# Starting the rotary tables earlier and pacing them by the attention that runs beside them

## The chip, the cores and the metric

The kernel runs on one core of one Trainium2 chip. The metric is device time in microseconds (us), the median of several runs. TensorE (PE in the profile) does the matrix products, VectorE (DVE) and ScalarE (ACT) the element-wise work, GpSimd (POOL) a share of it, and every transfer is issued from SyncE's queue (SP).

## What is computed

Two layers of a decoder trunk over 1024 positions of width 1024. Each layer normalises x, projects it to the inputs of eight heads of 256 (four mLSTM heads, four retention heads), runs them chunk by chunk, and projects back. Only the retention heads need the rotary tables, which depend on nothing but the positions:

```python
def rotary(t, positions):
    inv_freq = 1.0 / (ROPE_BASE ** jnp.linspace(0.0, 1.0, d // 2))
    ang = positions.astype(jnp.float32)[..., None] * inv_freq
    cos, sin = jnp.cos(ang), jnp.sin(ang)
    t1, t2 = jnp.split(t, 2, axis=-1)
    return jnp.concatenate([t1 * cos - t2 * sin, t2 * cos + t1 * sin], axis=-1)

def reference(...):
    for l in range(DEPTH):
        h = rmsnorm(x, norm_g[l]) * (1.0 + scale) + shift
        mq, mk, mv, mo, mz, mi, mf, rq, rk, rv, rz = split_cols(h @ w_in[l])
        ...   # y_m: four mLSTM heads from mq, mk, mv, mi, mf, gated by mo and mz
        ret = retention_chunkwise(rotary(rq, positions), rotary(rk, positions), rv)
        y_r = head_layernorm(ret) * silu(rz)
        x = x + gate * (concat(y_m, y_r) @ w_out[l])
    return rmsnorm(x, final_g)
```

## The kernel before

Float32 products are made of three products of split halves (`mm3`, lines 145 to 147): each operand is rounded to a high part by ScalarE (`split_to`, L621) and the rest is taken by GpSimd or VectorE (L622).

The program is written as generators. `run_units` runs the projections in the foreground; one step of it (a unit, some 12 to 24 matmuls) ends with `tick()`. `launch(gen, delay)` puts a background generator on a list, and each `tick` lets those that are due run to their next `yield n`, which asks for n ticks of rest. In this way an attention's products are dealt out among the next head's projections. TensorE's instructions stand in the order in which the program issues them (`manual_schedule` for PE). The order of the other engines' instructions is chosen by the build's scheduler, which may move an instruction ahead of its place in the program once its inputs are there; on the chip each engine then works its queue strictly in that order.

A head passes through `gate_path` (its z and o projections, evacuated by L550 and L560), `qk_ml` (q and k with a short convolution on VectorE, L636 to L644, and k's copies through memory, L663 to L673), `v_path` (values, split at L607 and L608) and `attention`. One round of an attention makes scores (matmuls L772; VectorE multiplies them by the decay matrix at L786, L787, L789 or L796, L797), values (L845, L855, then L859, L871 and `normalise`), and the update of the state: products into PSUM, added by VectorE into `cf` (L825), rounded by ScalarE to `cH` (L621), the rest by VectorE to `cL` (L622). The next round's values (L855) on TensorE wait for both.

PSUM banks of the pools `pp` (projections) and `pa` (attention), four each, are handed on in turn, so a matmul into a bank also waits for whoever read it last.

`rotary_tables` works in four rounds of 256 positions. A round loads the positions to all partitions (L381), makes the angle and its fraction of a turn in 26 instructions of VectorE on tiles of 128 x 256 (L383 to L407), and stores two results to memory (L410, `rdr`). It holds three of the six buffers named `g`. Its results are read back by `load_rotary` (L735) at the end of head 3's attention. It is launched once, in layer 0, behind head 1's values; head 1's attention is launched ahead of those values with a delay of 7 ticks.

Of the kernel before, what the change touches and what calls it, by code (L numbers as in the profile page):

```python
# [13 lines left out]
I32 = mybir.dt.int32  # L14
# [5 lines left out]
P = 128  # L20
# [8 lines left out]
CH = 256  # L29
# [38 lines left out]
def two_pi_split():  # L68
    c = 1.0 / (2.0 * math.pi)

    def top(v):
        m, e = math.frexp(v)
        return math.ldexp(round(m * 4096.0) / 4096.0, e)

    c1 = top(c)
    c2 = top(c - c1)
    return c1, c2, float(np.float32(c - c1 - c2))
# [3 lines left out]
def tile_hybrid_trunk(ctx, tc, x, xt, c, positions, w_ada, b_ada, norm_g, w_in, conv_w, conv_b,  # L81
                      b_igate, b_fgate, gn_m, gn_r, w_out, final_g, consts, out):
    nc = tc.nc
    V, A, G, PE, Q = nc.vector, nc.scalar, nc.gpsimd, nc.tensor, nc.sync
# [20 lines left out]
    def wt(tag, n, bufs, dt=F32):  # L105
        return wrk.tile([P, n], dt, tag=tag, bufs=bufs, name=nm(tag))
# [13 lines left out]
    def launch(gen, delay=0):  # L120
        uid[0] += 1
        pending.append([clock[0] + delay, uid[0], gen])
# [17 lines left out]
    def run_units(gen):  # L140
        for _ in gen:
            tick()
# [228 lines left out]

    rdr = [[dpool.tile([P, HALF], F32, name=f"rdr{i}{j}") for i in range(2)] for j in range(2)]

    def rotary_tables():
        c1, c2, c3 = two_pi_split()
        tiles = [wt("g", 512, 6) for _ in range(3)]
        ang, turn, tmp, rnd, a1, pos = (t[:, i * CH:(i + 1) * CH] for t in tiles for i in range(2))
        a2 = ang
        for n in range(4):
            i, cs = n // 2, slice((n % 2) * CH, (n % 2 + 1) * CH)  # L380
            Q.dma_start(pos.bitcast(I32), positions[0:1, n * CH:(n + 1) * CH].to_broadcast([P, CH]))  # L381
            yield 2
            V.tensor_copy(ang, pos.bitcast(I32))  # L383
            V.tensor_scalar(ang, ang, kc[:, C_FREQ:C_FREQ + 1], None, ALU.mult)
            V.tensor_copy(a1.bitcast(F32R), ang)
            yield 1
            V.tensor_tensor(a2, ang, a1, ALU.subtract)
            V.tensor_scalar(turn, a1, c3, None, ALU.mult)
            yield 1
            V.scalar_tensor_tensor(turn, a2, c3, turn, ALU.mult, ALU.add)  # L390
            V.scalar_tensor_tensor(turn, a2, c2, turn, ALU.mult, ALU.add)
            yield 1
            for src, cc in ((a1, c2), (a2, c1), (a1, c1)):
                V.tensor_scalar(tmp, src, cc, None, ALU.mult)
                V.tensor_scalar(rnd, tmp, MAG_I, -MAG_I, ALU.add, ALU.add)
                yield 1
                V.tensor_tensor(tmp, tmp, rnd, ALU.subtract)
                V.tensor_tensor(turn, turn, tmp, ALU.add)
                yield 1
            parts = ((1, 0.0, tmp), (0, 0.25, a1))  # L400
            for which, sh, dst in parts:
                if sh:
                    V.tensor_scalar(turn, turn, sh, None, ALU.add)
                V.tensor_scalar(rnd, turn, MAG_I, -MAG_I, ALU.add, ALU.add)
                V.tensor_tensor(dst, turn, rnd, ALU.subtract)
                yield 1
                V.tensor_scalar(dst, dst, 0.49999994, -0.49999994, ALU.min, ALU.max)  # L407
            yield 2
            for which, sh, dst in parts:
                Q.dma_start(rdr[which][i][:, cs], dst)  # L410
            yield 2
# [203 lines left out]
    def v0_splits(gt, vraw, vs):  # L615
        for j in range(NCH):
            vs.append(v_split(0, gt, vraw[j], j))
            yield 1
# [116 lines left out]
    def load_rotary(rot):  # L735
        for which in range(2):
            for i in range(2):
                t = wt("dm", 512, 2) if which == 0 else wt("nd", 516, 1) if i == 0 else wt("kw", 512, 1)
                Q.dma_start(t[:, 0:HALF], rdr[which][i])
                A.activation(t[:, 0:HALF], t[:, 0:HALF], AF.Sin, scale=2.0 * math.pi)  # L740
                rot[which].append(t[:, 0:HALF])

    def attention(l, hg, gt, qT, kT, kt, vs, gp, rot):
# [8 lines left out]
        def dm_load(j):  # L752
            if ml and j < NCH:
                dm = dms[j] = wt("dm", 512, 2)[:, 0:384]
                Q.dma_start(dm[:, 0:256], mdr[l][h:h + 1, j * CH:(j + 1) * CH].to_broadcast([P, CH]))
                if j in WHOLE:
                    Q.dma_start(dm[:, 256:384], mdr[l][h:h + 1, j * CH + P:(j + 1) * CH].to_broadcast([P, P]))

        def dm_make(j):
            if ml and j < NCH:  # L760
                dm = dms[j]
                for tt, (a, b) in enumerate(((0, 256), (256, 384)) if j in WHOLE else ((0, 128), (128, 256))):
                    G.affine_select(dm[:, a:b], dm[:, a:b], [[1, b - a]], ALU.is_ge, BIG, base=0, channel_multiplier=-1)
                    A.activation(dm[:, a:b], dm[:, a:b], AF.Exp, scale=-1.0, bias=gt["C4"][:, 2 * j + tt, 0, h:h + 1])
# [145 lines left out]
        def finish(j):  # L910
            half = j // 2
            if j % 2 == 0:
                st["z"] = wt("zt", 1024, 1)
            z5 = st["z"].rearrange("p (b t c) -> p t b c", b=8, c=32)[:, 2 * (j % 2):2 * (j % 2) + 2]
            V.transpose(z5, nrm[j].rearrange("p a (b c) -> p a b c", c=32))
            if j % 2 == 0:
                return
            for tb in range(4):
                last = Q.dma_start(ndr[l][hg][half][:, :, tb * P:(tb + 1) * P].rearrange("b j t -> j b t"),
                                   st["z"][tb * 32:(tb + 1) * 32, :].rearrange("p (b t) -> p b t", b=8))  # L920
            if hg == 3 and j == NCH - 1:
                with tc.issue_after(last.ins):
                    load_rotary(rot)

        if ml:
            dm_load(0)
            dm_load(1)
            yield 1
            dm_make(0)
            dm_make(1)  # L930
            yield 1
# [4 lines left out]
        for j in range(NCH):  # L936
            whole = j in WHOLE
            values(j, (0, 1) if whole else (0,))
            if whole:
                yield 1  # L940
            dm_make(j + 2)
            if j < NCH - 1:
                update((2 * j, 2 * j + 1) if whole else (2 * j,))
            yield 1
            if j + 2 < NCH:
                scores(j + 2)
            yield 1
            if not whole:
                values(j, (1,))
                update((2 * j + 1,))  # L950
                yield 1
            finish(j)
            yield 1

    class OutLoads:
        def __init__(self, l):
# [214 lines left out]
    for l in range(DEPTH):  # L1171
# [21 lines left out]
        if l == 0:  # L1193
# [7 lines left out]
            for step in script.split():  # L1201
                what, arg = step[0], step[1:]
                n = int(arg) if arg.isdigit() else 0
# [74 lines left out]
        for hg in range(8):  # L1278
            ml = hg < 4
            if hg == 0:  # L1280
                rot = [[], []]
            if hg > 0:
                gp = gp1 if hg == 1 else [[None, None], [None, None]]
                run_units(gate_path(l, hg, hT, gp, 0, 1 if hg == 7 else 2, hg > 1))
            vs = []
            kt = [None] * NCH
            kT = [[None, None], [None, None]]
            qT = [[None] * NCH, [None] * NCH]
            if hg == 4:
                run_units(v_path(l, hg, hT, gt, vs))  # L1290
            for which, res in ((0, qT), (1, kT)):
                if ml:
                    run_units(qk_ml(l, hg, which, hT, gt, kt, res))
                else:
                    run_units(qk_ret(l, hg % 4, which, hT, kt, res, *rot))
            if 0 < hg < 4:
                launch(attention(l, hg, gt, qT, kT, kt, vs, gp, rot), 4 if hg == 3 else 7)
            if hg not in (0, 4):
                run_units(v_path(l, hg, hT, gt, vs))
            if hg == 0:  # L1300
                launch(v0_splits(gt, vraw, vs), 1)
            if hg == 0 or hg > 3:
                launch(attention(l, hg, gt, qT, kT, kt, vs, gp, rot), 2 if hg == 0 else 0)
            if hg == 7:
                loads = OutLoads(l)
                for _ in gate_path(l, hg, hT, gp, 1):
                    loads.stage()
                    tick()
            if hg == 1 and l == 0:
                launch(rotary_tables(), 0)  # L1310
            if hg == 5:
                launch(gate_cols(l, gcol) if l == 0 else gate_rows(l, gb))
            if hg == 3 and l + 1 < DEPTH:
                launch(ada_columns_later(l + 1))
# [57 lines left out]
```

## Time and profile before

| what | value |
|---|---|
| three runs | 2303.51, 2303.7, 2304.77 us; median 2303.7 us |
| the profiled execution | 2305.89 us, of which 2304.2 us are the span from first to last instruction |
| TensorE busy | 2271.8 us, 99% of the span |
| VectorE, ScalarE, GpSimd busy | 1341.6 us (58%), 918.5 us (40%), 829.8 us (36%) |
| granted TensorE clock, mean | 0.997 |
| first position load issued, first to last table instruction of VectorE | 191.6 us; 293.7 to some 386.7 us |

In a row of the views the first entry is the line of the kernel, then engine and operation, then the tile written and the tile read. "[2.18 <-DVE th L787]" behind a row says that the engine stood idle for 2.18 us just before it and what ended that.

### The profile page before, as it was taken

What the parts mean: (1) busy time and instruction counts of PE and PEld (TensorE: products, weight loads), DVE (VectorE), ACT (ScalarE), POOL (GpSimd) and SP (SyncE); (2) the same over time, 40 slices, a digit from 0 to 9 for tenths busy, and PEclk for the clock granted to TensorE, in tenths of its full rate; (3) what the DMA queues carried; (4) which work ended last, traced back from release to release, by engine and by line L of the source; (5) the groups of instructions that cost most, each with busy time, mean ns of one, the idle gap of its engine ahead of it and who ended that gap; (6) DMA issues with size and microseconds to landing.
All of it is one profiled execution on the core that took longest, in us unless ns stands there. A gap on an engine that the chain in (4) does not pass through costs nothing. (4 is left out here: it accounts for less than half of the span.)

```text
span 2304.2 us, 34337 instructions
## 1 busy us (share of the span) xinstructions
PE 2271.8 (99%) x12415; PEld 1954.0 (85%) x12415; DVE 1341.6 (58%) x2823; ACT 918.5 (40%) x1768; POOL 829.8 (36%) x823
## 2 busy tenths in 40 slices
PE   6999999999999999999999999999999999999998
PEld 5888878889988888988888889888898888988886
DVE  7376688556555555585435675555564545557562
ACT  5535433444332323343544454344343323234442
POOL 1343434333343334224563434333334334341313
PEclk9999999999999999999999999999999999999999
DMA  8223232324433532376432323223223233436674
GB/s 258 78 66 99 73 84 81 80 76 116 115 110 92 151 97 78 120 257 208 166 109 71 80 75 82 78 75 78 70 70 97 74 92 88 124 85 212 176 246 118
DMA packets 360246, 259.45 MB, mean 113 GB/s; under 512 B 113266, under 2 KB 297338, under 8 KB 360076
## 3 DMA queue, kind: packets, MB, share of 16 engines
q1 hardware_dynamic: 360076, 257.26, 39.3%
q8 instruction: 97, 1.59, 0.3%
q14 instruction: 73, 0.60, 0.1%
HBM read 201.57 MB, written 55.61 MB: 112 GB/s over the span
## 5 line engine op out<-in xcount | busy, mean ns | idle before, releaser
L145 PE MATMUL pp<-b,wH 128*128 128x512 f32 x1824 | 721.5, 396 | 0.0
L147 PE MATMUL pp<-b,wL 128*128 128x512 f32 x1824 | 718.9, 394 | 0.0
L146 PE MATMUL pp<-b,wH 128*128 128x512 f32 x1824 | 717.8, 394 | 0.0
L622 POOL TENSOR_TENSOR wL<-raw,wH 128x512 fp32r<-128x512 f32 x338 | 453.4, 1351 | 544.3 <-ACT wH L621 491.4
L147 PEld LDWEIGHTS pp<-b,wL 128*128 128x128 f32 x1824 | 342.5, 188 | 81.6
L146 PEld LDWEIGHTS pp<-b,wH 128*128 128x128 f32 x1824 | 342.9, 188 | 72.9 <-issue 0.2
L145 PEld LDWEIGHTS pp<-b,wH 128*128 128x128 f32 x1824 | 342.8, 188 | 72.3 <-DVE g L550 0.3
L621 ACT CAST wH<-raw 128x512 fp32r<-128x512 f32 x402 | 245.7, 616 | 315.9 <-PE pp L146 114.1
L147 PE MATMUL pp<-wH,b 128*128 128x256 f32 (+1 forms) x1024 | 301.9, 295 | 0.0
L146 PE MATMUL pp<-wL,b 128*128 128x256 f32 (+1 forms) x1024 | 301.7, 295 | 0.0
L145 PE MATMUL pp<-wH,b 128*128 128x256 f32 (+1 forms) x1024 | 301.5, 294 | 0.0
L622 POOL TENSOR_TENSOR b<-acc,b 128x256 fp32r<-128x256 f32 (+1 forms) x192 | 176.0, 937 | 296.4 <-ACT b L621 281.4
L145 PEld LDWEIGHTS pp<-wH,b 128*128 128x128 f32 x1024 | 192.7, 188 | 6.2 <-DVE g L550 0.3
L146 PEld LDWEIGHTS pp<-wL,b 128*128 128x128 f32 x1024 | 192.6, 188 | 5.9
L147 PEld LDWEIGHTS pp<-wH,b 128*128 128x128 f32 x1024 | 192.5, 188 | 5.7
L639 DVE SCALAR_TENSOR_TENSOR acc<-pp,cols,acc 128x511 f32<-128x511 f32 (+2 forms) x192 | 142.5, 742 | 42.7 <-ACT acc L634 40.7
L621 ACT CAST b<-acc 128x256 fp32r<-128x256 f32 (+1 forms) x192 | 83.7, 476 | 179.7 <-DVE acc L716 128.5
L622 POOL TENSOR_TENSOR sL<-th,sH 128x256 fp32r<-128x256 f32 (+1 forms) x62 | 57.1, 921 | 208.0 <-ACT sH L621 158.8
L643 ACT ACTIVATE th<-acc 128x512 f32<-128x512 f32 x64 | 40.4, 632 | 143.4 <-DVE acc L641 78.1
L621 ACT CAST cH<-cf 128x516 fp32r<-128x516 f32 (+1 forms) x80 | 49.8, 622 | 107.4 <-DVE va L903 57.5
L622 DVE TENSOR_TENSOR wL<-raw,wH 128x512 fp32r<-128x512 f32 x64 | 44.3, 694 | 63.9 <-ACT wH L621 58.0
L145 PE MATMUL pa<-b,b 128*128 128x256 f32 (+1 forms) x256 | 72.3, 282 | 2.6 <-DVE th L787 2.2
(292 smaller groups left out, 3639.8 us busy)
## 6 DMA issues: line engine op xcount, KB each, us to landing
raw<-in_w_in_dram SPq DMA_DIRECT2D x274, 256.0 KB
raw<-in_w_out_dram SPq DMA_DIRECT2D x128, 256.0 KB
gdr<-g SPq DMA_DIRECT2D x64, 256.0 KB
ndr<-zt SPq DMA_DIRECT2D x128, 128.0 KB
raw<-in_w_ada_dram SPq DMA_DIRECT2D x64, 256.0 KB
g<-gdr SPq DMA_DIRECT2D x64, 256.0 KB
acc<-ndr SPq DMA_DIRECT2D x64, 256.0 KB
acc<-kdr SPq DMA_DIRECT2D x192, 64.0 KB
```

The costliest lines, as they stand in the source:

```text
L145: PE.matmul(o, lt[0], rt[0], start=start, stop=False)
L146: PE.matmul(o, lt[0], rt[1], start=False, stop=False)
L147: PE.matmul(o, lt[1], rt[0], start=False, stop=stop)
L621: A.copy(dst[0], src)
L622: eng.tensor_tensor(dst[1], src, f(dst[0]), ALU.subtract)
L639: V.scalar_tensor_tensor(acc[:, d:], pt[:, 0:HALF - d], wcol, acc[:, d:], ALU.mult, ALU.add)
L643: A.activation(th, acc, AF.Tanh, scale=0.5)
```

## The change

Three edits to `rotary_tables` and to its place. It is launched ahead of head 1's `v_path` (eight ticks earlier). Where it rested one tick between its small groups of instructions, it now rests two while an attention is running (a counter, `running`, that `attention` raises at its start and lowers at its end). And the positions of the next round are loaded as soon as this round's cast has read the buffer; the two ticks of rest behind each load are gone. No instruction is added or taken away.

```diff
+    running = [0]
     def rotary_tables():
...
+        def load(n):
+            if n < 4:
+                Q.dma_start(pos.bitcast(I32), positions[0:1, n * CH:(n + 1) * CH].to_broadcast([P, CH]))
+        def pace():
+            return 2 if running[0] else 1
+        load(0)
+        yield 1
         for n in range(4):
             i, cs = n // 2, slice((n % 2) * CH, (n % 2 + 1) * CH)
-            Q.dma_start(pos.bitcast(I32), positions[0:1, n * CH:(n + 1) * CH].to_broadcast([P, CH]))
-            yield 2
             V.tensor_copy(ang, pos.bitcast(I32))
+            load(n + 1)
             V.tensor_scalar(ang, ang, kc[:, C_FREQ:C_FREQ + 1], None, ALU.mult)
             V.tensor_copy(a1.bitcast(F32R), ang)
-            yield 1
+            yield pace()
...   (every other "yield 1" of the loop likewise)
@@ attention
+        running[0] += 1
         if ml:
             dm_load(0)
...
             finish(j)
             yield 1
+        running[0] -= 1
@@ the loop over the heads
             if 0 < hg < 4:
                 launch(attention(l, hg, gt, qT, kT, kt, vs, gp, rot), 4 if hg == 3 else 7)
+            if hg == 1 and l == 0:
+                launch(rotary_tables(), 0)
             if hg not in (0, 4):
                 run_units(v_path(l, hg, hT, gt, vs))
...
-            if hg == 1 and l == 0:
-                launch(rotary_tables(), 0)
```

More of the change, by code (lines that the diff above doesn't have):

```diff
@@ L378, in rotary_tables @@
         a2 = ang
+        def load(n):
[5 more added lines that the diff above has]
+        yield 1
         for n in range(4):
             i, cs = n // 2, slice((n % 2) * CH, (n % 2 + 1) * CH)
-            Q.dma_start(pos.bitcast(I32), positions[0:1, n * CH:(n + 1) * CH].to_broadcast([P, CH]))
-            yield 2
             V.tensor_copy(ang, pos.bitcast(I32))
+            load(n + 1)
             V.tensor_scalar(ang, ang, kc[:, C_FREQ:C_FREQ + 1], None, ALU.mult)
             V.tensor_copy(a1.bitcast(F32R), ang)
-            yield 1
+            yield pace()
             V.tensor_tensor(a2, ang, a1, ALU.subtract)
             V.tensor_scalar(turn, a1, c3, None, ALU.mult)
-            yield 1
+            yield pace()
             V.scalar_tensor_tensor(turn, a2, c3, turn, ALU.mult, ALU.add)
             V.scalar_tensor_tensor(turn, a2, c2, turn, ALU.mult, ALU.add)
-            yield 1
+            yield pace()
             for src, cc in ((a1, c2), (a2, c1), (a1, c1)):
@@ L395, in rotary_tables @@
                 V.tensor_scalar(rnd, tmp, MAG_I, -MAG_I, ALU.add, ALU.add)
-                yield 1
+                yield pace()
                 V.tensor_tensor(tmp, tmp, rnd, ALU.subtract)
                 V.tensor_tensor(turn, turn, tmp, ALU.add)
-                yield 1
+                yield pace()
             parts = ((1, 0.0, tmp), (0, 0.25, a1))
@@ L405, in rotary_tables @@
                 V.tensor_tensor(dst, turn, rnd, ALU.subtract)
-                yield 1
+                yield pace()
                 V.tensor_scalar(dst, dst, 0.49999994, -0.49999994, ALU.min, ALU.max)
```

## The prediction

> **What bounds the kernel now.** I read the page's engine shares first, then the table by stretches, then what TensorE waited for, and last the queues around the one stretch where it waited.
>
> ```profile
> span 2304.2 us, 34337 instructions
> PE 2271.8 (99%) x12415; PEld 1954.0 (85%) x12415; DVE 1341.6 (58%) x2823; ACT 918.5 (40%) x1768; POOL 829.8 (36%) x823
> 28.00:2290.00 2262.00, 2255.22 (x12361) 1941.53 (x12360) 1316.76 (x2771) 903.00 (x1734) 821.70 (x808) 1.00 0.39 110
> ```
>
> TensorE sets the time. Between the start-up and the last 14 us it is idle for 2262.00 - 2255.22 = 6.8 us, so no change to the tables can gain more than that. The table of stretches shows where they are made (columns: stretch, length, then busy time of PE, PEld, DVE, ACT, POOL).
>
> ```profile
> 200.00:212.00 12.00, 12.00 (x66) 10.27 (x65) 6.60 (x14) 6.05 (x14) 5.68 (x6) 1.00 0.30 83
> 212.00:234.00 22.00, 22.00 (x118) 18.86 (x117) 17.60 (x49) 10.94 (x22) 8.09 (x10) 1.00 0.31 79
> 293.00:313.00 20.00, 20.00 (x109) 17.25 (x108) 17.38 (x45) 7.87 (x19) 8.41 (x11) 1.00 0.28 66
> 313.00:336.00 23.00, 20.33 (x105) 16.66 (x105) 21.89 (x61) 8.20 (x17) 6.55 (x8) 1.00 0.33 89
> 336.00:360.00 24.00, 23.57 (x119) 19.49 (x118) 20.66 (x66) 9.30 (x17) 6.32 (x6) 1.00 0.35 95
> ...
> PE pa L145 <- DVE th L787: 2.2, 1, 2.2
> PE pa L145 <- ACT nd L859: 0.5, 1, 0.5
> PE pa L855 <- ACT cH L621: 0.4, 1, 0.4
> ```
>
> While head 1's attention runs, from 313 to 360 us, VectorE is busy 21.89 of 23 us and TensorE loses 2.67 + 0.43 = 3.1 us; the waits seen from 293 to 360 us (2.2, 0.5 and 0.4 us) are the same 3.1. The largest shows how it comes about:
>
> ```profile
> 318.37 1.44 POOL L622 TENSOR_TENSOR wL<-raw,wH 128x512 fp32r<-128x512 f32 x1 [2.58 <-ACT wH L621]
> ...
> 318.56 1.52 DVE L387 TENSOR_TENSOR g<-g,g 128x256 f32<-128x256 f32 x1
> ...
> 321.28 0.68 DVE L560 SCALAR_TENSOR_TENSOR g<-th,g 128x512 f32<-128x512 f32 x1
> ...
> 322.22 0.41 DVE L787 TENSOR_TENSOR th<-pa,dm 128x256 f32<-128x256 f32 x1
> ...
> 322.68 0.39 PE L145 MATMUL pa<-b,b 128*128 128x258 f32 x1 [2.18 <-DVE th L787]
> ```
>
> L787 frees a bank that TensorE wants, and it stands in VectorE's queue behind L387 and, in the rows left out, five more instructions of the tables, which nobody waits for here. L387 takes 1.52 us because it starts inside a GpSimd subtraction that ends at 318.37 + 1.44 = 319.81.
>
> **Step 1, what is removed.** The tables leave this stretch, and the 3.1 us of waiting should go. Its bounds: 0 if something else is as late, 6.8 if every idle moment of the middle were theirs. I take 3.1, since the rows name it.
>
> **Step 2, where the tables go.** The order in which the changed kernel's instructions are built, set against the old one, decides this. TensorE's order is the same, no engine has an instruction more, and beyond some 400 us all orders agree; what happens here is shifted to the end unchanged. But VectorE's queue does not begin the tables with head 1's values. The scheduler lifts the first cast (L383) to a place right behind the L796 multiply at 200.12 us, over 90 us earlier than the old 293.7:
>
> ```profile
> 200.12 0.68 DVE L796 TENSOR_TENSOR th<-pa,dm 128x512 f32<-128x512 f32 x1
> ```
>
> ```profile
> L383 DVE CAST g<-g x4: 270/282/289, 293.7 to 352.4; 128x256 f32<-128x256 int32 x4
> ```
>
> That is the middle of head 0's attention, beside head 1's o projections and convolutions. Of the 104 table instructions 21 stand ahead of the L786 multiply that used to run at 212.17, 42 ahead of the `cL` that used to run at 233.31, and 98 ahead of head 1's first scores at 291.68. The half pace therefore spares head 1's attention, but the tables now meet head 0's.
>
> **Step 3, what they cost there.** The price of one is read at the old place. The first row holds every VectorE instruction on a `g` tile from 293 to 336 us: 55 of the tables and four evacuations like the L560 above.
>
> ```profile
> 293.00:336.00 43.00, 25.82 (x59) 1.00 0.30 78
> ```
>
> ```profile
> L397 DVE TENSOR_TENSOR g<-g 128x256 f32<-128x256 f32 x12 | 5.5, 455 | 0.1
> L388 DVE TENSOR_SCALAR g<-g 128x256 f32<-128x256 f32 x4 | 1.2, 308 | 0.0
> ```
>
> (25.82 - 4 x 0.68) / 55 = 0.42 us; a successor starts a few hundredths before its forerunner ends, so 0.40. This includes what GpSimd holds up. From 200 to 234 us VectorE was busy 6.60 + 17.60 = 24.2 of 34 us, so 9.8 us are free, and 42 table instructions at 0.40 need 16.8. If every gap could be filled VectorE is 7.0 us late at the `cL` of 233.31. At 0.30 each (near L388's 0.308) it is 12.6 - 9.8 = 2.8 us, at 0.455 (L397's mean) 19.1 - 9.8 = 9.3. I take 0.40, the mean of the whole group.
>
> What is late there falls on TensorE almost at once:
>
> ```profile
> 233.31 0.69 DVE L622 TENSOR_TENSOR cL<-cf,cH 128x516 fp32r<-128x516 f32 x1
> ```
>
> ```profile
> 234.82 0.40 PE L855 MATMUL pa<-cL,b 128*128 128x258 f32 x2
> ```
>
> `cL` ends at 234.00 and TensorE reads it at 234.82: slack 0.8. So TensorE stands 7.0 - 0.8 = 6.2 us longer in head 0's attention (2.0 to 8.5). The convolutions behind it have banks to spare, and head 1's update, with no tables in front, has its old pace.
>
> **Step 4, two smaller terms.** The cast into `a1` (L385) waits until the store of the round before has read that buffer:
>
> ```profile
> L385 DVE CAST g<-g 128x256 fp32r<-128x256 f32 x4 | 1.2, 290 | 1.4 <-DMA rdr<-g 1.3
> ```
>
> It did so once for 1.3 us. In the new order seven short instructions stand between the clip and that cast, and behind the cast the normalisation and the next `cL` queue: 0.5 us, between 0 and 1.3. And head 1's first scores, L786, now stand ahead of the last value splits (L608), not behind them:
>
> ```profile
> 288.08 0.63 PE L772 MATMUL pa<-b,b 128*128 128x256 f32 x4
> 292.27 0.40 PE L145 MATMUL pp<-b,wH 128*128 128x512 f32 x1
> ```
>
> ```profile
> 289.97 1.65 DVE L608 SCALAR_TENSOR_TENSOR b<-pp,eul,b 128x256 fp32r<-128x256 f32 x4
> 291.68 0.41 DVE L786 TENSOR_TENSOR th<-pa,dm 128x256 f32<-128x256 f32 x1
> ```
>
> The splits cannot start before the scores are there at 288.08 + 0.63 = 288.7. Then come two multiplies and a table instruction (0.4 each), two halves of k (0.4 each), four splits (1.65) and some casts (0.3): 292.7, where TensorE took that bank at 292.27. That is 0.4 us, or 1.4 with one GpSimd hold; I take 1.0, between 0 and 2.0.
>
> **Step 5, what costs nothing.** Loading ahead gains nothing: the old load for the second round was already issued right behind the cast of 293.7, and the four casts show no idle time before them.
>
> ```profile
> 294.76 0.38 SPq L381 DMA_DIRECT2D g<-in_positions_dram  x1
> ```
>
> SyncE still issues four loads and eight stores. They move past weight loads and head 0's stores, at some 0.4 us of issue each, like this row; the queue is free there, and a weight load that waits for a table store behind VectorE is covered by the splits made ahead of TensorE. If that cover were gone it would be late by VectorE's own lateness, not by more. The three `g` buffers are held during the same two gate paths as before.
>
> **The sum.** 6.2 + 0.5 + 1.0 - 3.1 = +4.6 us on the profiled execution's 2305.9 us (span 2304.2). That one execution reads 2.2 us above the median of the runs, 2303.7; the difference carries over, so 2303.7 + 4.6 = 2308.3 us. About 0.2% (4.6 us) is what a measurement of this kernel can tell from no change; the forecast lies on that line. Its ends: 2.0 + 0 + 0 - 3.1 = -1.1 (2302.6) and 8.5 + 1.3 + 2.0 - 3.1 = +8.7 (2312.4).
>
> **A rule of the skill.** L387 above ended when GpSimd's instruction did. The Trainium skill (SBUF — State Buffer, Who interferes with whom) says that a VectorE instruction with two SBUF inputs, or a copy or tensor_scalar in a two-port mode, and a GpSimd instruction that reads SBUF share one port pair, and that the later one blocks fully until the other is done. The trace agrees (1.52 us against the 0.455 mean of its kind). By the rule moving such work does not free it; the third rival is that mechanism.
>
> **Rivals.**
>
> *Faster, because the gaps swallow it.* Head 0's attention shows no wait of TensorE, and 9.8 us of VectorE are free. If a table instruction costs 0.25 us or less when it stands between others, (9.8 + 0.8) / 42, nothing reaches TensorE and the 3.1 us are gained: 2300.6 us. Against it: L388's kind, the cheapest, averages 0.308.
>
> *The stall only changes place.* At 0.33 us each VectorE is 13.9 - 9.8 = 4.1 late and TensorE loses 3.3 us there, as much as it gains: 2303.7 us, give or take 1. Then the change does not do what it says; for it speaks that the tables again lie under one attention.
>
> *GpSimd's holds pile up.* From 200 to 234 us GpSimd has these to do:
>
> ```profile
> L622 POOL TENSOR_TENSOR wL<-raw,wH 128x512 fp32r<-128x512 f32 x5 | 6.9, 1382 | 11.6 <-ACT wH L621 10.5 <-issue 1.1
> L622 POOL TENSOR_TENSOR b<-acc,b 128x256 fp32r<-128x256 f32 x4 | 2.9, 739 | 5.2 <-ACT b L621 5.2
> L622 POOL TENSOR_TENSOR sL<-th,sH 128x256 fp32r<-128x256 f32 (+1 forms) x2 | 2.2, 1102 | 0.0
> ```
>
> 12.0 us in 34. With VectorE's queue never empty, most of them meet a table instruction. From 0.455 us each the upper end is reached: +8.7, 2312.4 us.
>
> **How the numbers follow.** My forecast, 0.50, half of it above the 0.2% line; faster 0.12, of which 0.02 by more than 0.2% (more of the 6.8 idle us would have to go); changed place 0.13; holds 0.25, slower. Slower: 0.25 + 0.27 = 0.52; faster by over 0.2%: 0.02; within: 0.46. The range takes the forecast's ends and those of the second and third rivals, 2302.5 to 2312.5, and leaves out the first.
>
> **What would show it.** After: no wait for L787 between 293 and 360 us, VectorE there well below 21.89 of 23; from 200 to 240 us VectorE full, and waits "PE pa L855 <- DVE cL" of some 6 us in all; a small wait of PE on L608 near the start of head 1's attention. I am wrong if TensorE is as dense as before from 200 to 250 us, or if it stops at the convolutions' banks (L639), which I gave no price.

## The result: 0.5% slower

| | before | changed |
|---|---|---|
| median of five runs each | 2304.15 us (2303.51 to 2304.77) | 2315.69 us (2315.32 to 2317.11) |
| ratio | | 1.0048, 95% interval 1.0037 to 1.0058 |
| profiled execution, its span | 2305.89 us, 2304.2 us | 2315.82 us, 2314.1 us |

The medians are 11.5 us apart, the two profiled executions 9.9 us; the forecast was +4.6, its range ended at 2312.5. In what follows a wait belongs to a profiled execution and a time is a median. The line numbers behind L380 are shifted: L608 is now L619, L622 is L633, L787 is L798, L855 is L866.

The profile of the changed kernel, first its page:

```profile
span 2314.1 us, 34332 instructions
PE 2276.1 (98%) x12415; PEld 1957.6 (85%) x12415; DVE 1337.4 (58%) x2823; ACT 918.5 (40%) x1768; POOL 830.8 (36%) x823
```

No engine has more instructions than before; TensorE's own busy time grew by 4.3 us with the same matmuls, so some of them ran slower. The table by stretches (length, then busy time of PE, PEld, DVE, ACT, POOL, then the granted clock of TensorE, the DMA share and GB/s):

```profile
200.00:212.00 12.00, 12.00 (x65) 10.30 (x64) 11.83 (x29) 5.68 (x13) 4.52 (x6) 1.00 0.38 104
212.00:234.00 22.00, 17.23 (x91) 14.09 (x91) 20.54 (x54) 8.56 (x18) 8.30 (x9) 1.00 0.33 82
234.00:293.00 59.00, 58.34 (x357) 51.81 (x356) 53.11 (x131) 24.49 (x48) 20.88 (x20) 1.00 0.30 78
293.00:313.00 20.00, 14.80 (x66) 12.30 (x66) 17.58 (x46) 6.28 (x17) 7.86 (x9) 0.83 0.34 70
313.00:336.00 23.00, 23.00 (x130) 20.02 (x129) 11.82 (x29) 9.53 (x20) 6.31 (x8) 1.00 0.37 93
336.00:360.00 24.00, 24.00 (x130) 20.64 (x129) 13.84 (x47) 9.81 (x19) 6.83 (x8) 1.00 0.28 68
```

TensorE's holes have moved from 313 to 360 us (now full, VectorE at 11.82 of 23 us) to two other places: 4.8 us in 212 to 234, foreseen, and 5.2 us in 293 to 313, where the granted clock was also only 0.83. What TensorE waited for from 195 to 400 us (sum, times, longest):

```profile
PE pp L145 <- DVE b L619: 5.9, 2, 5.2
PE pa L866 <- DVE cL L633: 2.2, 2, 2.1
PE pa L145 <- DVE th L798: 2.2, 1, 2.2
PE pa L866 <- ACT cH L632: 0.4, 1, 0.4
```

The last three are head 0's attention, the first is the value splits of head 1, which the forecast priced at 1.0. Its place on VectorE, what GpSimd did there, and its place on TensorE:

```profile
291.02 0.48 DVE L619 SCALAR_TENSOR_TENSOR b<-pp,eul,b 128x256 fp32r<-128x256 f32 x1
291.41 0.28 DVE L399 TENSOR_SCALAR g<-g 128x256 f32<-128x256 f32 x1
291.61 1.39 DVE L405 TENSOR_SCALAR g<-g 128x256 f32<-128x256 f32 x1
292.92 1.52 DVE L401 SCALAR_TENSOR_TENSOR g<-g 128x256 f32<-128x256 f32 x1
294.36 1.38 DVE L406 TENSOR_SCALAR g<-g 128x256 f32<-128x256 f32 x1
295.66 1.51 DVE L402 SCALAR_TENSOR_TENSOR g<-g 128x256 f32<-128x256 f32 x1
...
298.00 0.29 DVE L405 TENSOR_SCALAR g<-g 128x256 f32<-128x256 f32 x1
...
301.36 0.42 DVE L797 TENSOR_TENSOR th<-pa,dm 128x256 f32<-128x256 f32 x1
...
303.14 0.48 DVE L619 SCALAR_TENSOR_TENSOR b<-pp,eul,b 128x256 fp32r<-128x256 f32 x1
```

```profile
291.52 5.37 POOL L633 TENSOR_TENSOR wL<-raw,wH 128x512 fp32r<-128x512 f32 x4 [3.08 <-ACT wH L632]
```

```profile
298.40 1.10 PE L783 MATMUL pa<-b,b 128*128 128x256 f32 x8
304.71 0.80 PE L145 MATMUL pp<-b,wH 128*128 128x512 f32 x1 [5.20 <-DVE b L619]
305.30 0.63 PE L146 MATMUL pp<-b,wH 128*128 128x512 f32 x1
305.73 0.63 PE L147 MATMUL pp<-b,wL 128*128 128x512 f32 x1
```

Between the split of 291.02 and the one of 303.14 stand 16 instructions of the tables' fourth round in one row, up to L797 (a 17th follows). Four of them lie beside GpSimd's four subtractions and take 1.38 to 1.52 us (the same L405 takes 0.29 at 298.00); such an instruction is called held below. Nobody waits for the tables, but TensorE waits 5.2 us for the splits behind them. When TensorE goes on, its matmuls start 0.43 us apart instead of 0.23, twelve of them.

Setting each matmul against the same one before shows where the time went. "Late" is how much later it starts, each from its own first instruction; the places are on the old time scale.

| up to | late, us | this stretch added |
|---|---|---|
| head 0's second scores (213.6) | -0.2 | |
| end of head 0's attention (236) | 5.9 | +6.1 |
| first value projections of head 1 (292) | 7.1 | +1.2 |
| the wait for L619 and the slow matmuls behind it (296) | 15.2 | +8.1 (5.4 + 2.7) |
| end of head 1's attention (394) | 10.8 | -4.4 |
| last matmul | 9.9 | -0.9 (0.7 of it near 2130 us; the cause stays open) |

### The profile page after: what moved, and what is told of

Read it like the earlier page. It is cut to its first block, busy times and chain, and to the rows that moved or that the text cites. A ratio compares the mean times of both kernels' runs of the same rounds, so it can differ in the third digit from the quotient of the medians.

```text
span 2314.1 us, 34332 instructions
## 1 busy us (share of the span) xinstructions
PE 2276.1 (98%) x12415; PEld 1957.6 (85%) x12415; DVE 1337.4 (58%) x2823; ACT 918.5 (40%) x1768; POOL 830.8 (36%) x823
## 4 chain that ended last, share of the span: by engine, by line
PE 90%; DVE 4%; DMA 2%; ACT 1%; issue 1%; POOL 1%; SPq 1%; POOLq 0%; ACTq 0%; DVEq 0%
PE pp L145 23%; PE pp L147 23%; PE pp L146 23%; PE pa L146 4%; PE pa L147 4%; PE pa L145 4%; PE pa L866 3%; PE pa L783 2%; DMA b<-in_w_ada_dram 1%; DVE acc L650 1%; PE pa L856 1%; DMA b<-in_x_dram 0%; PE pp L1201 0%; PE pp L1202 0%; PE pp L1204 0%
## 5 line engine op out<-in xcount | busy, mean ns | idle before, releaser
L633 POOL TENSOR_TENSOR wL<-raw,wH 128x512 fp32r<-128x512 f32 x338 | 454.8, 1354 | 550.9 <-ACT wH L632 493.5
L633 POOL TENSOR_TENSOR b<-acc,b 128x256 fp32r<-128x256 f32 (+1 forms) x192 | 176.3, 939 | 299.1 <-ACT b L632 287.8
L633 POOL TENSOR_TENSOR sL<-th,sH 128x256 fp32r<-128x256 f32 (+1 forms) x62 | 56.3, 908 | 202.9 <-ACT sH L632 153.2
L633 DVE TENSOR_TENSOR wL<-raw,wH 128x512 fp32r<-128x512 f32 x64 | 44.3, 695 | 63.1 <-ACT wH L632 57.2
```

The lines of the kernel that those rows point to most:

```text
L633: eng.tensor_tensor(dst[1], src, f(dst[0]), ALU.subtract)
```

## The experiments

My theory: the whole cost is the place of the tables' instructions in VectorE's queue, in head 0's attention and ahead of head 1's value splits, there made worse by GpSimd and followed by a fallen clock. Rivals: the half pace, the earlier loads, the stores, a split that is late for another reason, or the value projections as such. Each run numbers its lines anew; the tiles keep their names.

**Which of the three edits counts.** Building each edit alone shows that the half pace and the earlier load, alone or together, leave every queue in the old order; the place of the launch alone gives the changed kernel's order on all engines but for two neighbours on SyncE. On the chip, `e1_place` is the kernel before with the launch alone moved. Set against the changed kernel, it takes back the half pace, as below, and the earlier load (in this diff and those that follow + is the experiment, and lines are left out):

```diff
-            yield pace()      # 2 while an attention runs
+            yield 1
```

> The launch alone is moved to head 1's value projections; the pace stays whole and a round's positions are loaded at its head. In the built program the table instructions then stand on VectorE's queue where they stand in the changed kernel (the first behind 266 other VectorE instructions, the last behind 415; before: 409 and 520). Theory 'place' (what costs is only where the table instructions stand in VectorE's queue): 2315.7 us, +11.5, with the same two waits of TensorE, 2.2 and 2.1 us in 212-234 and about 5.2 us near 299-305. Rival 'pace or loads' (the half pace or the load ahead has a part in the cost): several us away from 2315.7.

2317.0 us beside 2304.7 of before, ratio 1.0051 (1.0037 to 1.0065), and the same waits:

```profile
PE pp L145 <- DVE b L608: 5.9, 2, 5.2
PE pa L145 <- DVE th L787: 2.3, 1, 2.3
PE pa L855 <- DVE cL L622: 2.1, 1, 2.1
```

So the place of the launch is the whole change, and the two other edits do nothing that these runs can tell.

**Without the tables' work.** `x_notab` leaves three VectorE instructions a round and all loads and stores; `x_floor` leaves none of the instructions, no loads, and stores that write a constant. Neither makes the tables. The edit of `x_floor`:

```diff
-            V.tensor_copy(ang, pos.bitcast(I32))
-            ...                                    # 26 instructions and the load
+            yield 13
             for which in range(2):
-                Q.dma_start(rdr[which][i][:, cs], dst)
+                Q.dma_start(rdr[which][i][:, cs], quarter)
```

> The changed kernel without the tables' arithmetic: the four loads, three VectorE instructions a round instead of 26, and the eight stores stay, so the rotary tables are not computed. Theory 'VectorE work': both the cost of the change and the 3.7 us of waits in head 1's attention before are the tables' instructions on VectorE, so 2304.2 - 3.7 = 2300.4 us, TensorE without a wait of over 1 us between 195 and 400 us. Rival 'stores and loads' (SyncE's queue, the g buffers that the tables hold): stays above 2310.

2303.6 us, ratio 0.9992 (0.9983 to 1.0002): neither. Head 0's attention still had a wait, 1.7 us for the scores, because a few table instructions stood ahead of them waiting for transfers:

```profile
206.54 0.29 DVE L395 TENSOR_SCALAR g<-g 128x256 f32<-128x256 f32 x1 [1.68 <-DMA rdr<-g]
...
214.00 0.29 DVE L393 CAST g<-g 128x256 f32<-128x256 int32 x1 [1.16 <-DMA g<-in_positions_dram]
214.21 0.68 DVE L551 SCALAR_TENSOR_TENSOR g<-th,g 128x512 f32<-128x512 f32 x1
214.81 0.42 DVE L777 TENSOR_TENSOR th<-pa,dm 128x256 f32<-128x256 f32 x1
```

Twelve instructions are enough if one waits at the head of the queue. Hence the second one:

> The changed kernel with none of the tables' VectorE instructions and none of their loads: the eight stores write a constant, so the rotary tables are not computed. It mends x_notab, where the three instructions kept in each round stood at the head of VectorE's queue waiting for their round's load and for the round before's stores. Theory 'VectorE queue': TensorE has neither the wait for the scores of head 0's attention (2.2 us changed, 1.7 in x_notab) nor those of head 1's (3.7 us before): 2304.2 - 3.7 = 2300.5 us. Rival 'the wait in head 0's attention has another cause' : 2302.5 or more, with that wait still there.

2301.2 us beside 2305.0, ratio 0.9982 (0.9973 to 0.9991). From 195 us on to the end of head 1's attention TensorE shows no wait at all, and its lateness is -0.5 us up to 296 and -4.9 at 394. `x_floor` has no loads either, but `x_notab` has them and is not slower than before; so the changed kernel's loss is the tables' VectorE work. Some 4 us below before is about what the best placing of them can gain.

**The fourth round.** `x_pin4` holds the 26 instructions of round 4 behind head 1's last value split:

```diff
+        def pin(n):
+            return tc.issue_after(mark["head 1"].ins) if n == 3 else nullcontext()
...
-            V.tensor_copy(ang, pos.bitcast(I32))
+            with pin(n):
+                V.tensor_copy(ang, pos.bitcast(I32))
```

> The changed kernel with the 26 VectorE instructions of the fourth table round held behind the last value split of head 1; rounds 1 to 3 stay where the change put them. Theory 'queue position': the 5.2 us wait for L619 and the 2.6 us of slow matmuls behind it go, some 1 to 3 us come back as waits in head 1's attention, where round 4 now stands: 2307.5 to 2311. Rival 'the value splits are late for another reason' (ScalarE's copies or GpSimd's subtractions): no better than 2314.

2309.4 us, ratio 1.0020 (1.0011 to 1.0029). The wait for the split is 0.5 us, TensorE is full from 293 to 313 at full clock, and its lateness at 296 is 6.5 instead of 15.2:

```profile
293.00:313.00 20.00, 20.00 (x110) 17.13 (x109) 17.35 (x52) 9.67 (x23) 9.64 (x12) 1.00 0.40 96
```

Head 0's attention still costs its 6 us. What is left is close to the sum that the forecast had made: by the starts of the matmuls +6.0, +1.1 and -3.8 us, where it had 6.7, 1.0 and -3.1.

**Holds or count.** `x_hold` and `x_hold2` take GpSimd subtractions away from beside round 4; the weights that they belong to lose their low halves:

```diff
-            res += split_w(raw, n)
+            if low:
+                res += split_w(raw, n)
+            else:                                 # chosen z and o blocks of head 2, layer 0
...
+                A.copy(wH, raw)
+                G.memset(f(wL), 0.0)
```

> The changed kernel with the low halves of two weight blocks (head 2's first z and o blocks, layer 0) set to zero by GpSimd instead of subtracted, so those two projections lack their low halves. That takes away the four subtractions of 291.5 to 296.9 us beside which four of round 4's instructions took 1.4 to 1.5 us instead of 0.3 to 0.4. Theory 'holds': the wait of 5.2 us for L619 shrinks by about 4 us, TensorE's clock stays up behind it (another 2.6 us), so 2309 to 2311. Rival 'count' (16 instructions ahead of the splits cost it, held or not): wait still over 4 us, 2315 or more.

2312.2 us, ratio 1.0030 (1.0019 to 1.0041), between the two theories, because the edit reached only two of the four subtractions. The other two still held two instructions:

```profile
291.80 1.40 DVE L415 TENSOR_TENSOR g<-g,g 128x256 f32<-128x256 f32 x1
293.24 1.26 DVE L411 TENSOR_SCALAR g<-g 128x256 f32<-128x256 f32 x1
```

```profile
291.11 3.24 POOL L639 TENSOR_TENSOR wL<-raw,wH 128x512 fp32r<-128x512 f32 x2 [1.97 <-ACT wH L638]
```

> x_hold for all of head 2's z and o weight blocks (eight memsets in place of eight low halves, so those projections lack them): in x_hold two of the four subtractions of 291.5 to 296.9 us belonged to z's second block and stayed, and they still held two of round 4's instructions (1.40 and 1.26 us); its wait for the split fell from 5.2 to 2.9 us. Theory 'holds' (1.15 us a hold): with none left the wait is 0.5 to 1.0 us, no slow matmuls behind it, 2308 to 2310. Rival 'count': the wait stays near 2.9 us and the time near 2312.

2308.9 us, ratio 1.0016 (1.0006 to 1.0025), and the waits of the two kernels from 285 to 400 us, first with two subtractions left, then with none:

```profile
PE pp L145 <- DVE b L625: 3.0, 2, 2.9
```

```profile
PE pp L145 <- DVE b L625: 1.5, 2, 1.3
```

Its stretch of 293 to 313 us:

```profile
293.00:313.00 20.00, 18.72 (x104) 16.09 (x103) 16.57 (x51) 9.29 (x23) 4.64 (x9) 1.00 0.31 77
```

The wait goes 5.2, 2.9, 1.3 us with four, two and no subtractions. So 3.9 of its 5.2 us are holds, 1.3 the number of instructions, a little more than the 0.5 to 1.0 expected; without holds the clock stays up too (1.00 in the last row). The Trainium skill (SBUF — State Buffer, Who interferes with whom) gives the mechanism that the prediction weighed, one shared pair of ports, locked; held instructions of 1.38 to 1.52 us beside subtractions of 5.37 / 4 = 1.34 us, and of 1.26 and 1.40 beside those of 3.24 / 2 = 1.62 in `x_hold`, agree with it. That the ports are what holds them is argued; that they are held by GpSimd's subtractions is shown.

**The clock.** `x_fill` gives TensorE work during the wait:

```diff
+            if half and fill:
+                warm = ps_a()
+                for i in range(fill):
+                    PE.matmul(warm[:, 0:256], rmask[:, 0:P], rmask[:, 0:256], start=True, stop=True)
```

> The changed kernel with ten spare matmuls of a constant (128x256, f32) put on TensorE's queue right where it waits 5.2 us for L619; nothing reads their result. Theory 'clock' (the granted clock fell to 0.83 because TensorE stood idle, which makes 12 matmuls 0.43 us apart instead of 0.23): the wait becomes work, the matmuls behind it run 0.23 us apart, and the time falls by 2.6 us to 2313.1. Rival 'the matmuls behind the wait are slow for what they read or write': still 0.43 us apart, time unchanged or longer.

```profile
299.14 4.48 PE L368 MATMUL pa<-rmask 128*128 128x256 f32 x20
304.48 0.50 PE L145 MATMUL pp<-b,wH 128*128 128x512 f32 x1 [0.86 <-DVE b L624]
304.81 0.39 PE L146 MATMUL pp<-b,wH 128*128 128x512 f32 x1
305.04 0.40 PE L147 MATMUL pp<-b,wL 128*128 128x512 f32 x1
```

The matmuls behind the wait ran 0.23 us apart: it was the idling that made them slow. Yet the time stayed at 2317.0 us, ratio 1.0051 (1.0038 to 1.0064), since the added matmuls also made the scheduler put decay masks, which wait for GpSimd, ahead of the work on `nd` in ScalarE's queue, and TensorE then waited for L875:

```profile
PE pa L145 <- ACT nd L875: 2.3, 1, 2.3
```

`x_fill2` undoes that side effect:

> x_fill again, with three ScalarE instructions (the decay masks of the block after next) held behind the two copies of nd that they had overtaken there, so that ScalarE's order stands nearly as in the changed kernel. Theory 'clock': the twelve matmuls behind the wait again run 0.23 us apart, and now the time shows it: 2313 to 2314. Rival 'hidden' (the slow matmuls lie beside VectorE's and ScalarE's late work, and a wait takes their place, as in x_fill): 2315 to 2317, with a wait of 1 to 2.5 us between 313 and 340.

2315.2 us, ratio 1.0041 (1.0027 to 1.0055). The wait for `nd` is down to 0.2 us, and TensorE's lateness is 12.5 at 296 and 8.6 at 394, where the changed kernel has 15.2 and 10.8. The trace thus shows 2.2 to 2.7 us for the clock. The time is that of the rival "hidden", without the wait that it named (1 to 2.5 us): 10.2 us over before against 11.5 can't tell the 2.2 to 2.7 us from nothing, so they rest on one trace of each kernel.

**Where the tables do no harm.** Four kernels hold every table instruction in a chosen place. `y_prog` holds each behind the split, convolution, gate or transpose that the program has just issued, so the change does what its words say; `y_skip` also pauses while an attention runs; `y_conv` puts five or six behind each convolution of heads 1 to 3; `y_conv2` up to eight, but none behind the two convolutions ahead of the value splits. From `y_conv2`:

```diff
+            for op, args in ops(n):
+                with tc.issue_after(mark[0].ins):     # the last instruction of the convolution just issued
+                    op(*args)
+                left -= 1
+                if left == 0:
+                    yield                             # until the next convolution
```

> What the change's words say, with the built order made to follow: every table instruction is held behind the value split, convolution, gate or transpose that the program has just issued, so that the tables really begin with head 1's values and really go at half pace in head 1's attention and the ones behind. Theory 'queue position': no table in head 0's attention (5.7 us less than the changed kernel) and no row of 16 ahead of the splits (a further 6 to 8 us), but some tables among head 1's splits and in its attention, as in y_skip: 2304 to 2308. Rival 'place in the program' (starting with head 1's values costs it wherever the scheduler puts the instructions): 2312 or more.

> Each group of the tables' VectorE instructions is held behind the value split, convolution, gate or transpose that the program has just issued, the tables pause while an attention runs, and they begin with head 1. In the built order none stands in head 0's attention, and some ten behind a split stand in head 1's. Theory 'queue position': the waits of head 0's attention and of L619 are gone and most of head 1's too: 2300.5 to 2302, faster than before. Rival 'VectorE has no room elsewhere either' (the convolutions of the next projections are late): 2304 or more.

> The tables advance by five or six VectorE instructions behind each convolution of heads 1 to 3 (from the fifth of head 1 on), each held behind that convolution's last instruction, so that in the built order none stands in an attention's scores or state updates nor among the value splits; the positions are loaded ahead as in the change. Theory 'queue position': with no table instruction ahead of work that TensorE waits for, the waits of heads 0 and 1 go as in the kernel without tables (2301.2): 2301 to 2302.5, faster than before by 0.1 to 0.2%. Rival 'the convolutions have no room' (or the three g buffers held for longer stop the gates): 2304 or more, with waits of TensorE for L655's banks between 240 and 300, 350 and 410, 460 and 520 us.

> y_conv with the table instructions shifted away from the two key convolutions that stand right ahead of the value splits of heads 2 and 3, where y_conv's TensorE waited 2.0 us for L617 at 418 us and then ran 3.6 us of slow matmuls: none is queued behind those two, the earlier convolutions of heads 1 to 3 take eight each. Theory 'queue position': nothing that TensorE waits for stands behind a table instruction; 2301.5 to 2303, faster than before by 0.1 to 0.15%. Rival 'no room': eight instructions (2.8 us) a convolution are too many and the wait for the splits or for the convolutions' banks comes back: 2305 or more.

| | us | ratio to before | late at 236, 296, 394, 440 |
|---|---|---|---|
| `y_prog` | 2306.6 | 1.0005 (0.9996 to 1.0015) | 0.1, 2.5, -1.8, 0.6 |
| `y_skip` | 2307.2 | 1.0008 (0.9999 to 1.0016) | 0.1, 2.6, -1.8, 2.2 |
| `y_conv` | 2306.2 | 1.0006 (0.9997 to 1.0015) | -0.4, 1.2, -3.1, 0.7 |
| `y_conv2` | 2301.0 | 0.9980 (0.9971 to 0.9989) | -0.5, -0.1, -4.5, -4.5 |

None of the four is late at the end of head 0's attention. The first three still pay where tables stand ahead of splits. In `y_prog` and `y_skip` the first scores of heads 1 and 2 are split late; `y_skip`, 285 to 440 us:

```profile
PE pa L868 <- ACT sH L644: 2.7, 2, 1.4
PE pa L868 <- POOL sL L645: 1.2, 2, 0.6
```

In `y_conv` the last tables of head 2 stand between the key splits, and both the wait and the slow matmuls come back:

```profile
416.16 0.50 PE L145 MATMUL pp<-b,wH 128*128 128x512 f32 x1 [1.99 <-DVE b L617]
...
417.36 0.63 PE L146 MATMUL pp<-b,wH 128*128 128x512 f32 x1
417.78 0.63 PE L147 MATMUL pp<-b,wL 128*128 128x512 f32 x1
```

My numbers for `y_skip` and `y_conv` (2300.5 to 2302.5) were too good: I had left out who stands right behind the last group. `y_conv2` moved just those, and is 0.2% faster than before (4.7 us at the medians), as far as a kernel without the tables. In its rows TensorE has no hole where the others had theirs:

```profile
212.00:234.00 22.00, 22.00 (x118) 18.82 (x118) 17.26 (x48) 10.96 (x22) 8.27 (x11) 1.00 0.32 79
...
293.00:313.00 20.00, 20.00 (x110) 17.20 (x109) 9.48 (x25) 9.06 (x21) 7.30 (x10) 1.00 0.23 60
313.00:336.00 23.00, 23.00 (x127) 19.89 (x126) 14.32 (x38) 8.75 (x18) 6.20 (x8) 1.00 0.35 87
```

## Why the prediction was wrong

**Step 1** (3.1 us removed) was right and a little small: 4.4 us came back in head 1's attention, as in `x_floor`. The wait for L787 is gone and VectorE there is at 11.82 of 23 us, as named. The waits in the profile add up to less than the matmuls' starts show.

**Step 2** (the place in the queue) was right, and it carries everything: `e1_place`.

**Step 3** and the store's share of Step 4 (6.2 + 0.5) were right in size: 6.1 us; VectorE's wait for the store was 0.59 us where 0.5 had been put. The shape was not: I had put all of it on `cL` (L866), and 2.2 us of it were the scores, L798. The convolutions had banks to spare, as said.

**Step 4**, the scores ahead of the last splits, failed. It said 1.0 us, between 0 and 2.0, and the place cost 9.3: 1.2 + 5.4 of waiting and 2.7 of slow matmuls. The working let the splits wait for the scores, then "two multiplies and a table instruction"; it took VectorE to be free when the scores came. Step 2 had the count that denied this: 98 - 42 = 56 table instructions between the late `cL` and L797. The sum that Step 3 made for head 0's attention was not made for the stretch behind it. This row of the kernel before has it:

```profile
234.00:293.00 59.00, 59.00 (x370) 52.98 (x369) 38.41 (x85) 26.13 (x50) 22.31 (x20) 1.00 0.31 81
```

59 - 38.4 = 20.6 us free, 56 x 0.40 = 22.4 us to do: already 1.8 us too much, before any gap that can't be filled (VectorE was idle for 59 - 53.11 = 5.9 us of it in the changed kernel) and before the holds of 3.9 us. The average price of 0.40 has holds in it, but where four fall into one row ahead of a split the average doesn't show it. It was also too low here: by the reading that gave the prediction 0.42 us (all rows on `g` tiles, 239.2 to 301.4 us), one took 27.63 / 57 = 0.48.

**Step 5** (load, stores and buffers free) stands; no wait of TensorE names them. The clock was no step at all: the prediction put the slow matmuls at nothing, and they took 2.7 us in this execution.

**The rivals.** The holds' rival had the right mechanism and the wrong place: it looked from 200 to 234 us, where four of the 42 instructions took 1.09 to 1.28 us and the cost still came out as forecast; they bit at 291. The gaps did not swallow the tables, and the stall did not only change place.

**Smaller slips.** None of these moves the forecast. Between 293 and 336 us stand 54 table instructions and five evacuations, not 55 and four (the price stays 0.42). L388 is not the cheapest; L383 is, with 0.280 us, still above the first rival's 0.25. L387 ended 0.27 us behind GpSimd's subtraction, not with it. From the chances given to the four cases, slower is 0.50 and within the line 0.48, not 0.52 and 0.46.

## What to carry to other kernels

An instruction that nobody waits for costs what it delays: ask which split, copy or score stands next behind it in its queue, and sum up the free time of every stretch between its old and its new place, not only of the first. Where a scheduler may move work ahead, its place in the program and its pace there may mean nothing; read the built order, and pin the work behind an instruction if its place matters. When a stall of TensorE is priced, add the slow matmuls behind it.

## What the runs showed of the hardware

TensorE paid twice for a stop: after 5.2 us without work the next twelve matmuls of 512 columns started 0.43 us apart, not 0.23, about 2.5 us more; `x_fill` shows that it was the stop. Shorter waits did it in some runs and not in others: after 1.7 us in `x_notab` (granted clock 0.92 in its row from 212 to 234 us, below) and 1.99 in `y_conv`, but not after 2.2 in the changed kernel (1.00 in its row):

```profile
212.00:234.00 22.00, 20.28 (x102) 17.14 (x102) 16.97 (x46) 9.77 (x20) 7.42 (x10) 0.92 0.41 107
```

The Trainium skill (TensorE: Matmul & The Clock Gate, What's actually happening) puts the fall to half speed behind at least one idle window of some 3.4 us. The 5.2 us and the ratio of 0.43 to 0.23 agree; the falls after 1.7 to 2.0 us do not, and the measurement decides.

The traces also show what selects. In each of the fourteen traces the granted clock changes only at points that lie whole multiples of 3.41 us apart. In the changed kernel it is full from 30.75 us on, falls at 303.82, which is 80 x 3.413 us later, and is full again at 310.64. What counts is how long TensorE is idle within one such stretch, not how long a wait is:

| kernel | stretch, us | TensorE idle in it, us | granted clock in the next |
|---|---|---|---|
| changed | 300.40 to 303.82 | 3.41 | 0.50, and so in the one after |
| `x_hold` | 212.90 to 216.31 | 2.13 | 0.50 |
| `y_conv` | 413.56 to 416.98 | 1.99 | 0.50 |
| `x_notab` | 213.00 to 216.41 | 1.72 | 0.50 |
| `x_pin4` | 230.78 to 234.19 | 1.72 | 1.00 |
| changed | 211.65 to 215.07, and the next | 1.41, 0.75 | 1.00 |
| before | 318.20 to 321.61, and the next | 1.11, 1.07 | 1.00 |

Between 60 and 2290 us of them all, the nine stretches at full clock with 1.86 us of idle time or more are each followed by half a clock, none of those with 1.53 or less is, and of the five with 1.68 to 1.73 one is. So the border lies near 1.7 us, half of the stretch. The same wait in head 0's attention (2.2 and 2.1 us) was cut in two by such a point in the changed kernel and lay within one stretch in `x_hold`. Where the points lie differs from one execution to the next, so whether a wait of some 2 us costs slow matmuls is luck, and the 2.7 us behind the wait of 5.2 us are those of one execution.

In head 0's attention, where VectorE set the pace, the fall was free: `x_hold2` had a clock of 0.92 there (212 to 234 us) and was as late behind it as the changed kernel (5.7 against 5.9 us), with a wait for `cL` of 1.2 us instead of 2.1.
